# Gate scatter of a PEER layer: both gate parts side by side in one 256-column matmul, with PSUM divided anew for each stage

## Chip, cores, metric

One core of a Trainium2 chip runs the whole kernel. The metric is the device time of one execution in microseconds (us), as the median of several runs. Before the change it is 1055.61 us (three runs, 1055.03 to 1056.2).

## What is computed

The reference is one decoder layer on 256 tokens of width 1024: a mixing part (two attention branches, gated and merged), then a PEER part with 128 x 128 single-neuron experts, then a norm. Only the PEER part is touched:

```python
s = einsum('thpd,hpnd->thpn', qh, sub_keys)      # scores against 2 x 128 keys, 8 heads
sv, si = top_k(s, 16)                            # best keys, then best 16 pairs of them
expert_idx, gates = ...                          # 8 x 16 experts per token, softmax gates
hval = einsum('cd,chkd->chk', x, expert_u[expert_idx])
a = gates * gelu(hval)
out = einsum('chk,chkd->cd', a, expert_v[expert_idx])
```

## The kernel before

The kernel doesn't gather experts. It computes gelu(x @ u) for all 128 x 128 experts, multiplies by a matrix of gates that is zero where a token did not choose an expert, and multiplies the product by all of v. Experts are numbered (i, j); i counts 128 tiles, and j lies on the 128 partitions. Activations `act` are held as [j, i, token], in `act[0]` for i below N_PRE = 42 and in `act[1]` for the rest.

Products of full precision are made of three matmuls each (`mm3`, L93, L96, L97): both operands are split into a high part, rounded to fp32r, and the low rest. A weight block of 128 x 1024 comes by DMA into `raw`, ACT casts it to `hi` (L83), and DVE subtracts to get `lo` (L84); each has three buffers.

The stages in order: mixing part; the queries and scores of PEER (PQ, L573 to L585); the routing on DVE (`route`, top-k and index work), during which the first 42 up projections run; then the stage that matters here, the loop at L630 over i = 42 to 127; then the lower stage (`lower`, `v_step`, L655) with 12 matmuls of 512 columns for each of 128 blocks of v.

In the loop at L630 each i has one up projection (`up`, 24 matmuls of 256 columns into a PSUM tile `mm`) and `up_post`, which applies gelu: tokens that the scatter has not reached get the gelu written into `act` (L621), tokens that it has reached get it into `hg` (L624) and multiplied onto `act` (L625). In between, 64 calls of `scatter(t4, done)`, each for four tokens, are spread over the 86 values of i. A scatter builds the gate matrix of four tokens: `oh` (L602) holds one-hot rows of the expert numbers i and j, `gi` (L603) the one-hot of i times the gate, once for each of the two parts (high and low) into which a gate is split as f16. Both have the token innermost, so that one token's 128 columns are read in steps of four f16 elements. For each token, two matmuls of 128 columns (L606), one for each part, add up in PSUM, and give the gates as [j, i]. Four tokens fill one bank, a tile `tp`. DVE multiplies those of i below 42 onto `act[0]` (L608), those from 42 to `done` onto `act[1]` (L611), and ACT writes the others into `act[1]` (L613), where gelu will later be multiplied on.

PSUM has eight banks: four names (`mm`, `tp`, `sp`, `py`) with two each for the whole kernel. In the scatter stage `sp` and `py` lie idle; in the lower stage they are the four accumulators `acc`. At the lower stage's start ACT copies `ah` from `act` (L643) and DVE makes `al` (L644).

The order of instructions on each engine is set by the framework's scheduler, which goes by a modelled timeline; each engine then works through its queue strictly in order and waits on semaphores. All weight loads are issued on SP's queue; the change issues no DMA.

Of the kernel before, what the change touches and what calls it, by code (L numbers as in the profile page):

```python
# [9 lines left out]
F32 = mybir.dt.float32  # L10
F32R = mybir.dt.float32r
F16 = mybir.dt.float16
# [3 lines left out]
ALU = mybir.AluOpType  # L16
AX = mybir.AxisListType

P = 128
S = 256  # L20
# [9 lines left out]
NK = 128  # L30
# [9 lines left out]
G_SCALE = 2.0 ** 15  # L40
# [3 lines left out]
N_PRE = 42  # L44
# [7 lines left out]
def body(ctx, tc, x, g_mix, w_fb, w_va, w_qk, w_gate, w_f, b_f, w_br, w_out, g_ffn, w_pq,  # L52
         keys_t, u_t, v_e, g_fin, c_keep, c_mix, c_rot, c_sel, out, dbg=None):
    nc = tc.nc
# [4 lines left out]
    his = ctx.enter_context(tc.tile_pool(name="his", bufs=3))  # L59
    los = ctx.enter_context(tc.tile_pool(name="los", bufs=3))  # L60
    psum = ctx.enter_context(tc.tile_pool(name="psum", bufs=2, space=bass.MemoryType.PSUM))

    def bank(tag):
        return psum.tile([P, 512], F32, name=tag)

    def after(later, earlier):
        tc.add_manual_dep(
# [11 lines left out]
    def split(src, behind=None):  # L79
        r = load(src)  # L80
        h = his.tile([P, 1024], F32R, name="hi")
        l = los.tile([P, 1024], F32R, name="lo")
        ih = nc.scalar.copy(out=h, in_=r)  # L83
        il = nc.vector.tensor_tensor(out=l, in0=r, in1=h.bitcast(F32), op=ALU.subtract)  # L84
        lows.append(il)
        if behind is not None:
            for i, b in zip((ih, il), behind):
                if b is not None:
                    after(i, b)
        return h, l  # L90
# [25 lines left out]
    def norm_rstd(pool, src, tag, vector=(), cuts=(512, 1024)):  # L116

        rest = eps
        lo = 0
        for hi in cuts:  # L120
            ss = pool.tile([P, 1], F32, name="ss", bufs=8)
            piece = src[:, lo:hi]
            junk = bank(tag)[:, :hi - lo]
            if lo in vector:
                nc.vector.scalar_tensor_tensor(out=junk, in0=piece, scalar=1.0, in1=piece, op0=ALU.mult, op1=ALU.mult, accum_out=ss)
            else:
                nc.scalar.activation(out=junk, in_=piece, func=AF.Square, accum_out=ss)
            if hi < D:
                st = pool.tile([P, 1], F32, name="st", bufs=4)
                nc.vector.scalar_tensor_tensor(out=st, in0=ss, scalar=1.0 / D, in1=rest, op0=ALU.mult, op1=ALU.add)  # L130
                rest = st
            lo = hi
        sd = pool.tile([P, 1], F32, name="sd", bufs=4)
        nc.scalar.activation(out=sd, in_=ss, func=AF.Sqrt, scale=1.0 / D, bias=rest)
        rs = pool.tile([P, 1], F32, name="rs", bufs=4)
        nc.vector.reciprocal(out=rs, in_=sd)
        return rs
# [29 lines left out]
    def proj_t(src, xt, behind=None, tag="mm", late=False):  # L167
        w = split(src, behind)
        ps = bank(tag)[:, :S]
        if not late:  # L170
            for k in range(KD):
                mm3(ps, wk(w, k), [v[:, k] for v in xt], k == 0, k == KD - 1)
        else:

            for k in range(KD):
                for v in xt:
                    nc.tensor.matmul(ps, lhsT=wk(w, k)[0], rhs=v[:, k], start=k == 0 and v is xt[0], stop=False)  # L177
            for k in range(KD):
                nc.tensor.matmul(ps, lhsT=wk(w, k)[1], rhs=xt[0][:, k], start=False, stop=k == KD - 1)
        return ps  # L180


    with ExitStack() as fr:
# [5 lines left out]
        for t in range(NT):  # L189
            for n in range(2):  # L190
                sl = slice(n * 512, (n + 1) * 512)
# [23 lines left out]
        ps = bank("tp")[:HEADS, :S]  # L215
# [17 lines left out]
        for o in (0, 32, 64):  # L233
            part = ck[o:o + HEADS, P:]
# [6 lines left out]
        tp = bank("tp")  # L241
# [142 lines left out]
        for j2 in range(KD // 2):  # L384
# [3 lines left out]
            for jj in range(2):  # L388
                j = 2 * j2 + jj
                pp = []  # L390
                for w, yt, tag in ((wb, ys[0], "mm"), (wa, ys[1], "py")):
                    ps = bank(tag)[:, :S]
# [46 lines left out]
    ew = ctx.enter_context(tc.tile_pool(name="ew", bufs=2))  # L439
    pre = ctx.enter_context(tc.tile_pool(name="pre", bufs=1))  # L440
    act = [pre.tile([P, N_PRE, S], F32, name="act0")]

    def at(i):
        return act[0][:, i] if i < N_PRE else act[1][:, i - N_PRE]

    def up(i):
        ps = bank("mm")[:, :S]
        w = split(u_t[i])
        for k in range(KD):
            mm3(ps, wk(w, k), [a[:, k] for a in xt2], k == 0, k == KD - 1)  # L450
        return ps
# [99 lines left out]
    with ExitStack() as fr:  # L551
        tp_ = fr.enter_context(tc.tile_pool(name="tkp", bufs=1))
        tw = fr.enter_context(tc.tile_pool(name="tkw", bufs=2))
        kt = tp_.tile([P, 2 * PH * NK], F32, name="kt")
        nc.sync.dma_start(out=kt, in_=keys_t)
        val = tp_.tile([P, NT, 2 * PH, TOPK], F32, name="val")
        idx = tp_.tile([P, NT, 2 * PH, TOPK], U32, name="idx")
        scs = []
        steps = route(tp_, tw, val, idx, scs)
        debt = 0  # L560

        def spend(budget):
            nonlocal debt
            debt -= budget
            while debt < 0:
                c = next(steps, None)
                if c is None:
                    return False
                debt += c
            return True  # L570

        qhs = []
        for m in range(2 * PH):  # L573
            first = m < FIRST
            ps = proj_t(w_pq[m], xt2, (None if m == 0 else normed[0], normed[1]) if first else (qhs[m - FIRST], None), late=first)
            qh = tw.tile([P, S], F32, name="qh")
            qhs.append(nc.scalar.copy(out=qh, in_=ps))
            sp = bank("sp")[:, :NT * NK]
            for t in range(NT):
                nc.tensor.matmul(sp[:, t * NK:(t + 1) * NK], lhsT=qh[:, t * P:(t + 1) * P], rhs=kt[:, m * NK:(m + 1) * NK], start=True, stop=True)  # L580
            sc = tp_.tile([P, NT, NK], F32, name=f"sc{m}")
            nc.scalar.copy(out=sc, in_=sp.rearrange("p (t k) -> p t k", k=NK))
            scs.append(sc)
            if m > 0:
                spend(PQ_NS)  # L585

        for i in range(N_PRE):
            nc.scalar.activation(out=at(i), in_=up(i), func=AF.Gelu)  # L588
            spend(STEP_NS)
        for _ in steps:  # L590
            pass
    post = ctx.enter_context(tc.tile_pool(name="post", bufs=1))
    act.append(post.tile([P, NK - N_PRE, S], F32, name="act1"))

    def scatter(t4, done):

        ps = bank("tp")
        sl = slice(t4 * 4, t4 * 4 + 4)
        wide = [P, 2, NK, 4]
        oh = ew.tile(wide, F16, name="oh")  # L600
        gi = ew.tile(wide, F16, name="gi")
        nc.vector.tensor_tensor(out=oh, in0=iota.unsqueeze(1).to_broadcast(wide), in1=slot_e[:, :, sl].unsqueeze(2).to_broadcast(wide), op=ALU.is_equal)  # L602
        nc.vector.tensor_tensor(out=gi, in0=oh[:, 0].unsqueeze(1).to_broadcast(wide), in1=slot_g[:, :, sl].unsqueeze(2).to_broadcast(wide), op=ALU.mult)  # L603
        for q in range(4):
            for part in range(2):
                nc.tensor.matmul(ps[:, q * NK:(q + 1) * NK], lhsT=oh[:, 1, :, q], rhs=gi[:, part, :, q], start=part == 0, stop=part == 1)  # L606
        pv = ps.rearrange("p (q i) -> p i q", i=NK)
        nc.vector.scalar_tensor_tensor(out=act[0][:, :, sl], in0=pv[:, :N_PRE], scalar=1.0 / G_SCALE, in1=act[0][:, :, sl], op0=ALU.mult, op1=ALU.mult)  # L608
        d = done - N_PRE
        if d > 0:  # L610
            nc.vector.scalar_tensor_tensor(out=act[1][:, :d, sl], in0=pv[:, N_PRE:done], scalar=1.0 / G_SCALE, in1=act[1][:, :d, sl], op0=ALU.mult, op1=ALU.mult)  # L611
        if done < NK:
            nc.scalar.mul(out=act[1][:, d:, sl], in_=pv[:, done:], mul=1.0 / G_SCALE)  # L613

    last_gelu = []

# [13 lines left out]
    for i in range(N_PRE, NK):  # L630
        upto = -(-(i - N_PRE + 1) * n4 // (NK - N_PRE))
        while t4 < upto:
            scatter(t4, i)
            t4 += 1
        up_post(i, 4 * t4)

    acc = [[bank(tag) for _ in range(2)] for tag in ("py", "sp")]

    def lower(i):
        w = split(v_e[i])  # L640
        ah = ew.tile([P, S], F32R, name="ah", bufs=2)
        al = ew.tile([P, S], F32R, name="al", bufs=2)
        nc.scalar.copy(out=ah, in_=at(i))  # L643
        nc.vector.tensor_tensor(out=al, in0=at(i), in1=ah.bitcast(F32), op=ALU.subtract)  # L644
        return w, (ah, al)
# [49 lines left out]
    i = nc.vector.tensor_scalar(out=xg[0][:, halves[1]], in0=xg[0][:, halves[1]], scalar1=rs0, scalar2=None, op0=ALU.mult)  # L695
# [3 lines left out]
    for n, lo in enumerate((0, 256, 512, 768)):  # L699
        sl = slice(lo, lo + 256)  # L700
# [85 lines left out]
```

## Time and profile before

| | us |
|---|---|
| median of three runs | 1055.61 |
| the profiled execution | 1059.37 |
| its span, first to last instruction | 1057.6 |
| PE busy | 1040.5 |
| DVE busy | 740.6 |
| ACT busy | 546.1 |
| scatter stage, first to last scatter matmul | 388.5 to 696.7 |

PE is TensorE's matmuls, PEld its weight loads (they overlap with matmuls), DVE is VectorE, ACT ScalarE. Busy time is the union of an engine's instruction records. A matmul's record is longer than the distance between two matmuls, since they are pipelined; what one costs is read from the distance between starts, or from its share of the chain of waits over its count. The chain of waits is followed back from the end: at each step to what released an instruction or to the one before it on its engine. The granted clock of TensorE is 0.993 of full speed in the mean.

### The profile page before, as it was taken

How to read it: one execution, taken by the hardware profiler on the slowest of the kernel's cores; microseconds unless marked ns; L12 is line 12 of the kernel's file. 1: busy time of each engine (PE TensorE's matmuls, PEld its weight loads, DVE VectorE, ACT ScalarE, POOL GpSimd, SP SyncE). 2: the span in 40 equal slices, each digit the busy share in tenths (PEclk: the TensorE clock that was granted, in tenths of full speed). 3: DMA queues.
4: the chain of work that ended last, by engine and by line, in shares of the span. 5: the costliest groups of instructions: out<-in, count | busy, mean ns of one | idle time of the engine just before them, and what ended most of it. 6: DMA issues, size and time to landing. Idle time of an engine off the chain costs nothing.

```text
span 1057.6 us, 18493 instructions
## 1 busy us (share of the span) xinstructions
PE 1040.5 (98%) x7076; PEld 953.7 (90%) x7076; DVE 740.6 (70%) x1479; ACT 546.1 (52%) x983; POOL 6.9 (1%) x12
## 2 busy tenths in 40 slices
PE   7999999989999999999999999999999999999997
PEld 5888999989999999999999999998888888888886
DVE  4566546679999986677777788866566656656665
ACT  5555566454554544444444444455555555555554
POOL 1000000000000000000000000000000000000001
PEclk8999999999999999999999999999999999999999
DMA  6544435544566564545455444556666666666663
GB/s 206 172 139 118 123 120 175 186 169 151 167 190 189 177 186 150 158 142 155 146 151 149 146 152 142 157 163 197 189 193 198 192 190 195 196 190 193 198 193 126
DMA packets 49959, 177.84 MB, mean 168 GB/s; under 512 B 5752, under 2 KB 6648, under 8 KB 49744
## 3 DMA queue, kind: packets, MB, share of 16 engines
q1 hardware_dynamic: 49104, 175.62, 54.9%
q8 instruction: 55, 0.90, 0.4%
q10 hardware_dynamic: 432, 0.66, 0.2%
q0 software_dynamic: 336, 0.40, 0.2%
q14 instruction: 32, 0.26, 0.1%
HBM read 175.60 MB, written 1.05 MB: 167 GB/s over the span
## 4 chain that ended last, share of the span: by engine, by line
PE 95%; DVE 3%; DMA 1%; ACT 0%; issue 0%; SPq 0%; ACTq 0%
PE mm L93 16%; PE mm L96 15%; PE mm L97 15%; PE py L93 6%; PE py L97 6%; PE py L96 6%; PE tp L606 6%; PE sp L93 6%; PE sp L97 6%; PE sp L96 6%; PE sp L312 1%; PE mm L177 1%; DVE lo L84 1%; DMA cst<-in_c_keep_dram 1%; PE sp L580 1%; PE tp L327 1%
## 5 line engine op out<-in xcount | busy, mean ns | idle before, releaser
L84 DVE TENSOR_TENSOR lo<-raw,hi 128x1024 fp32r<-128x1024 f32 x328 | 400.2, 1221 | 145.7 <-ACT hi L83 143.8
L83 ACT CAST hi<-raw 128x1024 fp32r<-128x1024 f32 x328 | 344.8, 1053 | 256.2 <-PE mm L96 142.0
L93 PE MATMUL mm<-xt2h,hi 128*128 128x256 f32 x1128 | 325.8, 289 | 0.8 <-ACT act L588 0.8
L97 PE MATMUL mm<-xt2h,lo 128*128 128x256 f32 x1128 | 317.5, 281 | 0.5 <-DVE lo L84 0.5
L96 PE MATMUL mm<-xt2l,hi 128*128 128x256 f32 x1128 | 317.2, 281 | 0.0
L93 PEld LDWEIGHTS mm<-xt2h,hi 128*128 128x128 f32 x1128 | 214.3, 190 | 1.6 <-ACT act L588 1.0
L97 PEld LDWEIGHTS mm<-xt2h,lo 128*128 128x128 f32 x1128 | 212.7, 189 | 0.9 <-DVE lo L84 0.9
L96 PEld LDWEIGHTS mm<-xt2l,hi 128*128 128x128 f32 x1128 | 213.6, 189 | 0.0
L643 ACT CAST ah<-act 128x256 fp32r<-128x256 f32 x128 | 52.0, 407 | 95.2 <-PE sp L96 95.1
L644 DVE TENSOR_TENSOR al<-act,ah 128x256 fp32r<-128x256 f32 x128 | 54.3, 425 | 60.0 <-PE sp L97 59.1
L96 PE MATMUL py<-lo,ah 128*128 128x512 f32 x256 | 79.9, 390 | 0.0
L93 PE MATMUL py<-hi,ah 128*128 128x512 f32 x256 | 79.7, 390 | 0.0
L97 PE MATMUL py<-hi,al 128*128 128x512 f32 x256 | 79.6, 389 | 0.0
L96 PE MATMUL sp<-lo,ah 128*128 128x512 f32 x254 | 79.0, 389 | 0.0
L93 PE MATMUL sp<-hi,ah 128*128 128x512 f32 x254 | 78.9, 389 | 0.0
L97 PE MATMUL sp<-hi,al 128*128 128x512 f32 x254 | 78.7, 389 | 0.0
L606 PE MATMUL tp<-gi,oh 128*128 128x128 f16 x512 | 74.8, 296 | 0.0
L613 ACT ACTIVATE act<-tp 128x344 f32<-128x344 f32 (+31 forms) x64 | 20.3, 318 | 86.6 <-DVE act L611 80.8
L608 DVE SCALAR_TENSOR_TENSOR act<-tp,act 128x168 f32<-128x168 f32 x64 | 21.2, 332 | 56.1 <-PE tp L606 56.1
L93 PE MATMUL mm<-xt1h,hi 128*128 128x256 f32 x208 | 60.4, 290 | 0.0
L97 PE MATMUL mm<-xt1h,lo 128*128 128x256 f32 x208 | 59.5, 286 | 0.0
L96 PE MATMUL mm<-xt1l,hi 128*128 128x256 f32 x208 | 59.3, 285 | 0.0
(259 smaller groups left out, 1408.0 us busy)
## 6 DMA issues: line engine op xcount, KB each, us to landing
raw<-in_u_t_dram SPq DMA_DIRECT2D x128, 512.0 KB, 3.5
raw<-in_v_e_dram SPq DMA_DIRECT2D x128, 512.0 KB, 3.5
raw<-in_w_gate_dram SPq DMA_DIRECT2D x16, 512.0 KB, 3.6
raw<-in_w_pq_dram SPq DMA_DIRECT2D x16, 512.0 KB, 3.7
raw<-in_w_fb_dram SPq DMA_DIRECT2D x8, 512.0 KB, 4.7
raw<-in_w_va_dram SPq DMA_DIRECT2D x8, 512.0 KB, 3.5
raw<-in_w_qk_dram SPq DMA_DIRECT2D x8, 512.0 KB, 3.6
raw<-in_w_br_dram SPq DMA_DIRECT2D x8, 512.0 KB, 3.5
```

The source lines that it names most:

```text
L83: ih = nc.scalar.copy(out=h, in_=r)
L84: il = nc.vector.tensor_tensor(out=l, in0=r, in1=h.bitcast(F32), op=ALU.subtract)
L93: i = nc.tensor.matmul(ps, lhsT=lhs[0], rhs=rhs[0], start=start, stop=False)
L96: nc.tensor.matmul(ps, lhsT=lhs[0], rhs=rhs[1], start=False, stop=False)
L97: return nc.tensor.matmul(ps, lhsT=lhs[1], rhs=rhs[0], start=False, stop=stop)
L177: nc.tensor.matmul(ps, lhsT=wk(w, k)[0], rhs=v[:, k], start=k == 0 and v is xt[0], stop=False)
L312: nc.tensor.matmul(sp[:, o:o + n], lhsT=q[:, t * P:(t + 1) * P], rhs=k[:, :n], start=not fox, stop=not fox or t == 1)
L606: nc.tensor.matmul(ps[:, q * NK:(q + 1) * NK], lhsT=oh[:, 1, :, q], rhs=gi[:, part, :, q], start=part == 0, stop=part == 1)
L608: nc.vector.scalar_tensor_tensor(out=act[0][:, :, sl], in0=pv[:, :N_PRE], scalar=1.0 / G_SCALE, in1=act[0][:, :, sl], op0=ALU.mult, op1=AL ...
L613: nc.scalar.mul(out=act[1][:, d:, sl], in_=pv[:, done:], mul=1.0 / G_SCALE)
L643: nc.scalar.copy(out=ah, in_=at(i))
L644: nc.vector.tensor_tensor(out=al, in0=at(i), in1=ah.bitcast(F32), op=ALU.subtract)
```

## The change

Each token's two matmuls (128 columns each, adding up in PSUM) become one matmul of 256 columns: the left operand is the same, the right one is both parts of `gi` side by side, and the result lies in PSUM as two halves, `hi` and `lo`. So the tile of four tokens (`lay`) takes two banks. The halves are added while they are read: ACT copies the scaled low half to SBUF (`gl`), DVE adds the scaled high half, in `gl` for i below `done` and straight into `act[1]` for the rest, and then multiplies `gl` onto `act[0]` and `act[1]`.

The PSUM is divided by stage: `mm` and `tp` stay as they are; `sp` and `py` (four banks) are given up before the scatter stage, where two tiles `lay` take their place, and the lower stage opens four accumulators there again. `oh`, `gi` and `gl` lie in a pool of the scatter stage (`lw`), `ah` and `al` in one of the lower stage (`dw`); before they lay in `ew`, which was open from the routing on.

```diff
     psum = ctx.enter_context(tc.tile_pool(name="psum", bufs=2, space=bass.MemoryType.PSUM))
+    mixing = ExitStack()
+    psum2 = mixing.enter_context(tc.tile_pool(name="psum2", bufs=2, space=bass.MemoryType.PSUM))
     def bank(tag):
-        return psum.tile([P, 512], F32, name=tag)
+        return (psum2 if tag in ("sp", "py") else psum).tile([P, 512], F32, name=tag)
...
+    mixing.close()
     post = ctx.enter_context(tc.tile_pool(name="post", bufs=1))
+    laying = ExitStack()
+    lw = laying.enter_context(tc.tile_pool(name="lw", bufs=2))
+    psum3 = laying.enter_context(tc.tile_pool(name="psum3", bufs=2, space=bass.MemoryType.PSUM))
...
     def scatter(t4, done):
-        ps = bank("tp")
+        ps = psum3.tile([P, 4, 2, NK], F32, name="lay")
         sl = slice(t4 * 4, t4 * 4 + 4)
         wide = [P, 2, NK, 4]
-        oh = ew.tile(wide, F16, name="oh")
-        gi = ew.tile(wide, F16, name="gi")
+        oh = lw.tile(wide, F16, name="oh")
+        gi = lw.tile(wide, F16, name="gi")
...
         for q in range(4):
-            for part in range(2):
-                nc.tensor.matmul(ps[:, q * NK:(q + 1) * NK], lhsT=oh[:, 1, :, q], rhs=gi[:, part, :, q], start=part == 0, stop=part == 1)
-        pv = ps.rearrange("p (q i) -> p i q", i=NK)
-        nc.vector.scalar_tensor_tensor(out=act[0][:, :, sl], in0=pv[:, :N_PRE], scalar=1.0 / G_SCALE, in1=act[0][:, :, sl], op0=ALU.mult, op1=ALU.mult)
+            nc.tensor.matmul(ps[:, q], lhsT=oh[:, 1, :, q], rhs=gi[:, :, :, q], start=True, stop=True)
+        hi, lo = (ps[:, :, z].rearrange("p q i -> p i q") for z in range(2))
+        gl = lw.tile([P, NK, 4], F32, name="gl")
+        nc.scalar.mul(out=gl, in_=lo, mul=1.0 / G_SCALE)
         d = done - N_PRE
+        nc.vector.scalar_tensor_tensor(out=gl[:, :done], in0=hi[:, :done], scalar=1.0 / G_SCALE, in1=gl[:, :done], op0=ALU.mult, op1=ALU.add)
+        if done < NK:
+            nc.vector.scalar_tensor_tensor(out=act[1][:, d:, sl], in0=hi[:, done:], scalar=1.0 / G_SCALE, in1=gl[:, done:], op0=ALU.mult, op1=ALU.add)
+        nc.vector.tensor_tensor(out=act[0][:, :, sl], in0=gl[:, :N_PRE], in1=act[0][:, :, sl], op=ALU.mult)
         if d > 0:
-            nc.vector.scalar_tensor_tensor(out=act[1][:, :d, sl], in0=pv[:, N_PRE:done], scalar=1.0 / G_SCALE, in1=act[1][:, :d, sl], op0=ALU.mult, op1=ALU.mult)
-        if done < NK:
-            nc.scalar.mul(out=act[1][:, d:, sl], in_=pv[:, done:], mul=1.0 / G_SCALE)
+            nc.vector.tensor_tensor(out=act[1][:, :d, sl], in0=gl[:, N_PRE:done], in1=act[1][:, :d, sl], op=ALU.mult)
...
-    acc = [[bank(tag) for _ in range(2)] for tag in ("py", "sp")]
+    laying.close()
+    psum4 = ctx.enter_context(tc.tile_pool(name="psum4", bufs=2, space=bass.MemoryType.PSUM))
+    dw = ctx.enter_context(tc.tile_pool(name="dw", bufs=2))
+    acc = [[psum4.tile([P, 512], F32, name=tag) for _ in range(2)] for tag in ("py", "sp")]
     def lower(i):
         w = split(v_e[i])
-        ah = ew.tile([P, S], F32R, name="ah", bufs=2)
-        al = ew.tile([P, S], F32R, name="al", bufs=2)
+        ah = dw.tile([P, S], F32R, name="ah")
+        al = dw.tile([P, S], F32R, name="al")
```

## Rows read from the trace of the kernel before

**Rows 1.** The page: busy time by engine, and PE's slices in tenths.

```profile
PE 1040.5 (98%) x7076; PEld 953.7 (90%) x7076; DVE 740.6 (70%) x1479; ACT 546.1 (52%) x983; POOL 6.9 (1%) x12
...
PE   7999999989999999999999999999999999999997
```

**Rows 2.** Stretches of 50 us: length; busy PE, PEld, DVE, ACT, POOL; clock; DMA.

```profile
390.00:440.00 50.00, 50.00 (x424) 49.38 (x423) 32.88 (x62) 22.94 (x49) 0.00 (x0) 1.00 0.52 158
440.00:490.00 50.00, 50.00 (x423) 49.26 (x422) 36.20 (x72) 23.55 (x53) 0.00 (x0) 1.00 0.49 148
490.00:540.00 50.00, 50.00 (x424) 49.28 (x423) 36.34 (x69) 23.14 (x54) 0.00 (x0) 1.00 0.50 149
540.00:590.00 50.00, 50.00 (x423) 49.28 (x422) 38.70 (x72) 22.96 (x54) 0.00 (x0) 1.00 0.50 148
590.00:640.00 50.00, 50.00 (x424) 49.31 (x423) 38.58 (x69) 22.16 (x53) 0.00 (x0) 1.00 0.51 150
640.00:690.00 50.00, 50.00 (x424) 49.34 (x423) 41.39 (x72) 20.83 (x53) 0.00 (x0) 1.00 0.50 148
```

**Rows 3.** Chain of waits from 390 to 690 us, shares by line.

```profile
by line: PE mm L93 26.9%; PE mm L96 26.8%; PE mm L97 26.7%; PE tp L606 19.6%
```

**Rows 4.** Groups by line on PE, 390 to 690 us: busy, mean ns | idle.

```profile
L93 PE MATMUL mm<-xt2h,hi 128*128 128x256 f32 x681 | 198.5, 292 | 0.0
...
L606 PE MATMUL tp<-gi,oh 128*128 128x128 f16 x491 | 71.8, 296 | 0.0
```

**Rows 5.** Records of lines L606 and L200: ns min/median/max, first and last start.

```profile
L606 PEld LDWEIGHTS <-oh x512: 111/117/141, 388.4 to 696.6; 128*128 128x128 f16 x171
L606 PE MATMUL tp<-gi,oh x512: 280/297/303, 388.5 to 696.7; 128*128 128x128 f16 x171
...
L200 PE MATMUL py<-wz x14: 379/622/635, 1.2 to 5.9; 128*128 128x512 f16 x14
```

**Rows 6.** Timeline of PEld near 561 us: start us, length us.

```profile
561.17 0.35 PEld L606 LDWEIGHTS <-oh 128*128 128x128 f16 x4
```

**Rows 7.** A stretch of 100 us in the lower stage, columns as in rows 2.

```profile
800.00:900.00 100.00, 100.00 (x443) 82.85 (x442) 60.42 (x75) 53.87 (x74) 0.00 (x0) 1.00 0.64 192
```

**Rows 8.** Groups by line and shape, whole span: busy us, mean ns | idle before.

```profile
L608 DVE SCALAR_TENSOR_TENSOR act<-tp,act 128x168 f32<-128x168 f32 x64 | 21.2, 332 | 56.1 <-PE tp L606 56.1
...
L625 DVE TENSOR_TENSOR act<-act,hg 128x168 f32<-128x168 f32 x1 | 0.3, 323 | 0.0
...
L292 ACT COPY v<-mm 128x512 f32<-128x512 f32 x4 | 2.3, 586 | 2.4 <-PE mm L97 2.4
```

**Rows 9.** Timeline of DVE at the end of the scatter stage.

```profile
697.30 1.22 DVE L84 TENSOR_TENSOR lo<-raw,hi 128x1024 fp32r<-128x1024 f32 x1
698.44 0.50 DVE L611 SCALAR_TENSOR_TENSOR act<-tp,act 128x336 f32<-128x336 f32 x1
698.86 0.41 DVE L625 TENSOR_TENSOR act<-act,hg 128x252 f32<-128x252 f32 x1
699.18 0.42 DVE L644 TENSOR_TENSOR al<-act,ah 128x256 fp32r<-128x256 f32 x1
```

**Rows 10.** Waits from 390 to 690 us: us in total, times, longest.

```profile
DVE act L608 <- PE tp L606: 53.2, 57, 1.5
DVE lo L84 <- ACT hi L83: 21.2, 26, 2.3
```

**Rows 11.** Timelines of DVE and PE in the middle of the stage.

```profile
567.41 0.68 DVE L603 TENSOR_TENSOR gi<-oh,slot_g 128x1024 f16<-128x1024 f16 x1
...
571.61 1.11 PE L606 MATMUL tp<-gi,oh 128*128 128x128 f16 x8
```

**Rows 12.** Timelines of PE at the end of the scatter stage.

```profile
696.72 0.30 PE L606 MATMUL tp<-gi,oh 128*128 128x128 f16 x1
...
702.53 0.40 PE L93 MATMUL py<-hi,ah 128*128 128x512 f32 x1
```

**Rows 13.** Records of line L602.

```profile
L602 DVE TENSOR_TENSOR oh<-iota,slot_e x64: 675/681/693, 342.0 to 686.9; 128x1024 f16<-128x1024 f16 x64
```

## The prediction, made before the changed kernel ran

> **What bounds the kernel now.** I read the page first: PE is busy 98% of the span and DVE 70%, and PE's slices show no hole between start and end [rows 1]. A busy PE need not be a limiting PE, so next the stretches in which the scatter runs: from 390 to 690 us PE is busy 50.00 of every 50 us at full granted clock, while DVE climbs from 32.88 to 41.39 and ACT falls from 22.94 to 20.83 [rows 2]. Then the chain of waits there: it stays on PE throughout. The scatter matmuls (L606) own 19.6% of it, 58.8 us for 491 instructions, which is 119.8 ns each; the up projection's (L93, L96, L97, 2041 in all, 681 of them L93) own 80.4%, 118.2 ns each [rows 3, 4]. So time leaves this stage only through PE, and DVE has little room left before it is the next limit.
>
> **The matmuls.** Gone: 512 matmuls of 128 columns at 119.8 ns, 61.3 us of chain. New: 256 matmuls of 256 columns. Whether that halves the cost depends on what the 119.8 ns pay for.
> The weight load does not look like it. It is listed with 117 ns, but four loads in a row span 0.35 us, so the fourth starts 0.23 us after the first, 78 ns apart: they overlap, run ahead, and then wait for matmuls that come every 119.8 ns [rows 5, 6].
> Streaming does. A scatter matmul reads every fourth f16 element of gi, in steps of 8 bytes, and its 128 columns take as long as 256 dense columns of the up projection, 118.2 ns; its record has 297 ns, where a dense f16 one of 512 columns has 379 at best [rows 5]. A strided column seems to cost two dense ones. The nearest row for 256 strided columns is then the 512-column matmul of the lower stage: 443 in 100 us, 225.7 ns [rows 7]. Bounds: 119.8 ns if the old price buys 256 columns as well (30.7 us in all, a gain of 30.6), and twice 119.8 (no gain). I take 225.7 plus the 1.6 ns by which the strided one exceeds its dense twin, 227.3 ns: 58.2 us, **-3.1 us**. Per scatter that is 0.909 against 0.958, 0.05 us less.
> [...]
>
> **DVE.** L608 and L611 read PSUM and multiply in one pass. After, two sums read hi (512 elements together, split at "done"), and two multiplies read gl in SBUF, with the element counts of L608 and L611. The multiplies cost what the old passes did: 168 elements take 332 ns from PSUM (L608) and 323 from SBUF (L625) [rows 8]. The two sums come on top. L608 with 168 elements and L611 with 336 differ by 0.17 us, 1.0 ns per element; back to back L611 holds the engine 0.42 us (698.44 to 698.86), so about 0.08 is fixed [rows 8, 9]. The sums cost 512 x 1.0 ns + 2 x 0.08 = **0.67 us** per scatter, 43 us over 64. Bounds: 0.59 (one fixed part hidden) and 0.84 (both paid at record length, 332 - 168 ns fixed).
> What covers them is DVE's idle time. 491 matmuls in 300 us are 10.2 scatters per 50 us, so DVE gets 6.9 us more in each stretch: 39.8, 43.1, 43.2, 45.6, 45.5, 48.3. PE needs 50 - 10.2 x 0.05 = 49.5. Even the last stretch fits, with 1.2 us to spare: **0**, but the cover is nearly used up.
>
> **ACT and the new wait.** L613 becomes one copy of 512 elements from PSUM, 586 ns by L292 [rows 8]; even with nothing taken off for L613 that is 6 us per stretch in an engine idle for 26 us or more of every 50 [rows 2]: 0. New is that DVE waits for ACT's gl, where L608 waited for PE (53.2 us in all, 0.86 per scatter) [rows 10]. Behind the waiting sum on DVE stand oh, the next lo and gi, and PE waits for lo and gi. On ACT gl and the hi casts stand in one queue, so either can hold the other for one cast. Today gi is ready well ahead: made from 567.41 to 568.09, its eight matmuls start at 571.61 [rows 11]. These 3.5 us pay for single late sums: 0 here; the other end is the second rival.
>
> **Pools, and the end of the stage.** The PSUM that lay takes was last read in the PQ stage, before the routing: 0. acc and ah now wait until the last scatter lets go. Before, the last scatter matmul starts at 696.72, al runs from 699.18 to 699.60, and PE reaches the first lower matmul at 702.53 [rows 9, 12]. The copy (0.59) and two sums (0.67) move al's end to 700.9, and with one more lo in front (698.44 minus its start at 697.30, 1.14) to 702.0 [rows 9]: still in time, 0; bound 1 us. oh and gi move to a pool opened after the routing, where the first oh was made at 342 us [rows 13]. If two pairs must now come after it, some 2.7 us of DVE leave the crowded routing stretch for the first scatter stretch, which has 9.7 to spare: 0, within 1 us either way.
>
> **Sum.** The profiled execution took 1059.4 us, its span 1057.6; the median of the runs shown is 1055.6, 3.8 below it. 1059.4 - 3.1 + 0 + 0 + 0 = 1056.3; carried to the median, **1052.5 us**. A measurement of this kernel tells about 0.2% (2.1 us) from no change.
>
> **The rivals.**
> *Gain eaten, no change.* If each scatter's sum still waits 0.35 us for gl, DVE needs 3.6 us more per 50: the last stretch misses by 2.4 us, and with a stage end 0.5 us late the gain is gone: 1055.4. The same comes out at 239.6 ns per matmul. For it: lo alone waits 21.2 us for hi already [rows 10]. Against it: DVE waits today because it is ahead.
> *DVE becomes the limit, slower.* The place is the first sum of each scatter, in order behind PE and ACT. It decides from some 0.38 us of wait per scatter on, where the fourth and fifth stretch are full too (3.9 us / 10.2). At 0.6 us (6.1 per stretch) the last three miss by 2.2, 2.1 and 4.9 us: 9.2 - 3.1, 1061.7. With today's 0.86 kept, some 1075. For it: 48.3 of 49.5 late in the stage, and one engine more in the chain. Against it: a DVE that is late finds gl done.
> *The stride is free, much faster.* At 119.8 ns PE needs 45.1 us per old 50, and DVE takes over in the last three stretches (45.6, 45.5, 48.3): 25 us saved, 1030; with 0.35 us of wait per scatter 11 us, 1044; I name 1036. Against it stands that 128 strided columns cost what 256 dense ones do. [...]
>
> **How the numbers follow.** Forecast 1052.5, chance 0.42 (own range 1051 to 1054); gain eaten 0.26; DVE the limit 0.22; free stride 0.10. A twentieth, from the first, lands inside 0.2%: faster 0.47, same 0.31, slower 0.22. The range holds the first two whole and the DVE case up to 0.6 us of wait, and goes down to 1046 for a stride that is only partly dear (a fifth of the way to the far bound); the free stride (0.10) and the far DVE tail (0.07) are left out: 1046 to 1062.
>
> **What would show it.** Right: the new matmuls come about 227 ns apart, PE is busy 50 of 50 from 390 us to the stage's end, DVE near 45 in the mean and 48 late, and its waits for gl are short. Wrong: PE idle before L93 or L97 with DVE's lo as releaser, or before the scatter matmuls with gi; matmuls 120 ns apart; a hole on PE near 700 us.

## The result, and the profile after

The changed kernel takes **1073.11 us** (median of four runs, 1071.78 to 1074.59) against 1055.32 for the kernel before beside it: a ratio of **1.0167, 95% interval [1.0155, 1.018]**, slower by 17.8 us. That lies outside the range of 1046 to 1062. The profiled execution took 1074.59 us, its span 1072.6.

The page of the changed kernel, as in [rows 1]: PE's busy share is the same 98%, with 256 matmuls fewer, and DVE has 41.5 us more. Line numbers shift by the change: L93, L96 and L97 become L95, L98 and L99, the scatter matmul L606 becomes L611, `oh` is L608, `gl` L614, the two sums are L616 and L618, the two multiplies L619 and L621, the gelu L629 and L632.

```profile
PE 1052.4 (98%) x6820; PEld 936.1 (87%) x6820; DVE 782.1 (73%) x1607; ACT 559.7 (52%) x983; POOL 6.9 (1%) x12
```

The stretches, with the columns of [rows 2, 7] (length; busy PE, PEld, DVE, ACT, POOL; clock; DMA), show three places:

```profile
390.00:440.00 50.00, 50.00 (x386) 46.26 (x386) 40.06 (x85) 25.50 (x53) 0.00 (x0) 1.00 0.54 167
...
540.00:590.00 50.00, 50.00 (x386) 46.44 (x385) 43.66 (x88) 25.63 (x55) 0.00 (x0) 1.00 0.51 156
590.00:640.00 50.00, 48.34 (x368) 43.88 (x366) 43.95 (x86) 24.23 (x51) 0.00 (x0) 1.00 0.49 150
640.00:690.00 50.00, 48.27 (x363) 43.70 (x364) 44.85 (x87) 23.27 (x50) 0.00 (x0) 1.00 0.45 138
690.00:720.00 30.00, 26.39 (x144) 22.46 (x144) 18.52 (x35) 14.16 (x25) 0.00 (x0) 0.89 0.38 122
...
800.00:900.00 100.00, 100.00 (x432) 81.09 (x431) 59.00 (x73) 52.52 (x72) 0.00 (x0) 1.00 0.60 188
```

*The lower stage.* PE is busy without a gap at full clock, as before, and yet only 432 matmuls start in 100 us where 443 did [rows 7]: 231.5 ns each for 225.7. Over the stage's 1536 matmuls these 5.8 ns make 8.9 us, half of the loss, in a stage whose matmuls the change doesn't touch.

*The late scatter stage.* From 590 to 690 us PE has 3.4 us of idle time, where it had none. *The end of that stage.* From 690 to 720 us 3.6 us are missing, and the mean granted clock is 0.89 (it was 1.00 before). The waits from 385 to 720 us (us in total, times, longest):

```profile
DVE oh L608 <- PE lay L611: 32.1, 49, 1.5
DVE lo L86 <- ACT hi L85: 13.6, 20, 1.9
ACT gl L614 <- PE lay L611: 11.2, 7, 3.4
...
ACT gl L614 <- DVE act L621: 5.5, 5, 1.3
...
PE mm L95 <- ACT hg L632: 3.6, 5, 1.0
PE py L95 <- ACT ah L654: 3.4, 1, 3.4
```

The two PE waits are new. The first is the up projection waiting for a PSUM tile `mm` that gelu has not read. ACT's timeline there (start us, length us, idle before) shows why gelu is late:

```profile
630.48 0.21 ACT L629 ACTIVATE act<-mm 128x56 f32<-128x56 f32 x1
630.59 0.59 ACT L614 ACTIVATE gl<-lay 128x512 f32<-128x512 f32 x1
633.35 1.05 ACT L85 CAST hi<-raw 128x1024 fp32r<-128x1024 f32 x1 [2.17 <-PE mm L98]
634.30 0.21 ACT L629 ACTIVATE act<-mm 128x52 f32<-128x52 f32 x1
634.41 0.59 ACT L614 ACTIVATE gl<-lay 128x512 f32<-128x512 f32 x1
634.89 0.33 ACT L632 ACTIVATE hg<-mm 128x200 f32<-128x200 f32 x1
```

One tile's gelu is in two parts: 56 tokens at 630.48 and the other 200 at 634.89, 4.4 us later, with two `gl` and a `hi` that waits for PE in between. `mm` has two buffers, so PE stops (0.96 us there, until 635.28).

The second wait is the hole before the first lower matmul. DVE's timeline:

```profile
700.96 0.68 DVE L616 SCALAR_TENSOR_TENSOR gl<-lay,gl 128x504 f32<-128x504 f32 x1
701.55 0.15 DVE L618 SCALAR_TENSOR_TENSOR act<-lay,gl 128x8 f32<-128x8 f32 x1
703.58 1.22 DVE L86 TENSOR_TENSOR lo<-raw,hi 128x1024 fp32r<-128x1024 f32 x1 [1.88 <-ACT hi L85]
704.73 0.33 DVE L619 TENSOR_TENSOR act<-gl,act 128x168 f32<-128x168 f32 x1
704.97 0.50 DVE L621 TENSOR_TENSOR act<-gl,act 128x336 f32<-128x336 f32 x1
```

and PE's:

```profile
702.30 0.28 PE L99 MATMUL mm<-xt2h,lo 128*128 128x256 f32 x1
706.02 0.79 PE L95 MATMUL py<-hi,ah 128*128 128x512 f32 x1 [3.43 <-ACT ah L654]
706.61 0.63 PE L98 MATMUL py<-lo,ah 128*128 128x512 f32 x1
707.03 0.63 PE L95 MATMUL py<-hi,ah 128*128 128x512 f32 x1
```

The last scatter's sums are done at 701.7, but a `lo` for the lower stage stands between them and the multiplies. It waits 1.88 us for its `hi` (which waits 1.95 us for a buffer that PE reads up to its last up projection), so the multiplies end at 705.5, and `ah` needs them. After 3.43 us of idle time the lower stage starts at half the granted clock (0.50 from 706.0 to 711.7 us, where it was 1.00 from 690 to 702): its first matmuls are 0.43 us apart, up to 711.7, and 0.23 later.

### The profile page after: what moved, and what is told of

The parts are those of the page before. It is cut to its first block, busy times and chain, and to the rows that moved or that the text cites. A ratio compares the mean times of both kernels' runs of the same rounds, so it can differ in the third digit from the quotient of the medians.

```text
span 1072.6 us, 18119 instructions
## 1 busy us (share of the span) xinstructions
PE 1052.4 (98%) x6820; PEld 936.1 (87%) x6820; DVE 782.1 (73%) x1607; ACT 559.7 (52%) x983; POOL 6.9 (1%) x12
## 5 line engine op out<-in xcount | busy, mean ns | idle before, releaser
L95 PE MATMUL mm<-xt2h,hi 128*128 128x256 f32 x1128 | 328.5, 291 | 3.6 <-ACT hg L632 3.6
L98 PE MATMUL mm<-xt2l,hi 128*128 128x256 f32 x1128 | 318.1, 282 | 0.0
L99 PE MATMUL mm<-xt2h,lo 128*128 128x256 f32 x1128 | 318.1, 282 | 0.0
L95 PEld LDWEIGHTS mm<-xt2h,hi 128*128 128x128 f32 x1128 | 213.6, 189 | 11.9 <-ACT hg L632 5.8
L98 PEld LDWEIGHTS mm<-xt2l,hi 128*128 128x128 f32 x1128 | 213.6, 189 | 1.6
L99 PEld LDWEIGHTS mm<-xt2h,lo 128*128 128x128 f32 x1128 | 212.8, 189 | 0.7
L95 PE MATMUL py<-hi,ah 128*128 128x512 f32 x256 | 81.9, 398 | 3.4 <-ACT ah L654 3.4
L98 PE MATMUL py<-lo,ah 128*128 128x512 f32 x256 | 81.7, 397 | 0.0
L99 PE MATMUL py<-hi,al 128*128 128x512 f32 x256 | 81.0, 396 | 0.0
L98 PE MATMUL sp<-lo,ah 128*128 128x512 f32 x254 | 80.7, 396 | 0.0
L95 PE MATMUL sp<-hi,ah 128*128 128x512 f32 x254 | 80.7, 396 | 0.0
L99 PE MATMUL sp<-hi,al 128*128 128x512 f32 x254 | 80.2, 396 | 0.0
L611 PE MATMUL lay<-gi,oh 128*128 128x256 f16 x256 | 69.5, 407 | 0.0
L608 DVE TENSOR_TENSOR oh<-iota,slot_e 128x1024 f16<-128x1024 f16 x64 | 44.1, 690 | 32.3 <-PE lay L611 32.1
L95 PEld LDWEIGHTS py<-hi,ah 128*128 128x128 f32 x256 | 48.7, 190 | 15.0 <-ACT ah L654 3.6
L95 PE MATMUL mm<-xt1h,hi 128*128 128x256 f32 x208 | 60.4, 290 | 0.0
L99 PE MATMUL mm<-xt1h,lo 128*128 128x256 f32 x208 | 59.5, 286 | 0.0
L98 PE MATMUL mm<-xt1l,hi 128*128 128x256 f32 x208 | 59.2, 285 | 0.0
```

What stands on the lines that cost most here:

```text
L95: i = nc.tensor.matmul(ps, lhsT=lhs[0], rhs=rhs[0], start=start, stop=False)
L98: nc.tensor.matmul(ps, lhsT=lhs[0], rhs=rhs[1], start=False, stop=False)
L99: return nc.tensor.matmul(ps, lhsT=lhs[1], rhs=rhs[0], start=False, stop=stop)
L611: nc.tensor.matmul(ps[:, q], lhsT=oh[:, 1, :, q], rhs=gi[:, :, :, q], start=True, stop=True)
```

## The experiments

Fourteen kernels ran; e1, e8 and e11 to e14 were timed four times or more, the others once. The first three asked for the lower stage. In the diffs `...` stands for lines not shown.

**e1.** Before, with `ah` and `al` alone moved to a pool of their own above everything else, as the change places them.

```diff
+    dw = ctx.enter_context(tc.tile_pool(name="dw", bufs=2))
...
-        ah = ew.tile([P, S], F32R, name="ah", bufs=2)
-        al = ew.tile([P, S], F32R, name="al", bufs=2)
+        ah = dw.tile([P, S], F32R, name="ah")
+        al = dw.tile([P, S], F32R, name="al")
```

> The kernel before, with one thing of the change: ah and al lie in a pool opened after act1, so at the top of SBUF (byte 224384 of a partition on) in place of 92672. In the changed kernel the lower stage's matmuls of 512 columns come 231.4 ns apart (432 to 433 in 100 us), before 225.7 (443). Theory A (where ah and al lie sets that pace): 432 to 434 matmuls in 100 us of the lower stage, some 8 us slower in all, about 1063.5. Theory B (the accumulators' PSUM banks) and theory C (something the scatter stage leaves behind, or the single execution): 442 to 444 in 100 us, the time of before.

1063.77 us, ratio 1.0074 [1.0057, 1.009]. The stretch in the lower stage:

```profile
800.00:900.00 100.00, 100.00 (x432) 81.09 (x431) 59.05 (x73) 52.22 (x72) 0.00 (x0) 1.00 0.63 188
```

This edit alone brings the 432, and costs 7.6 us over the kernel before measured beside it (1056.13). So about half of the loss is where two small tiles lie in SBUF.

**e2.** Before, with `sp` and `py` in a PSUM pool of their own, opened as in the changed kernel, which moves `py` to other banks.

```diff
+    psum2 = ctx.enter_context(tc.tile_pool(name="psum2", bufs=2, space=bass.MemoryType.PSUM))
...
-        return psum.tile([P, 512], F32, name=tag)
+        return (psum2 if tag in ("sp", "py") else psum).tile([P, 512], F32, name=tag)
```

> The kernel before, with another single thing of the change: sp and py in a PSUM pool of their own, which moves the accumulators py from banks 0 and 1 to banks 4 and 5, as in the changed kernel. Theory A (place of ah and al): 443 matmuls in 100 us of the lower stage. Theory B (PSUM banks): 432 to 434.

1054.04 us, 443 matmuls per 100 us: the banks change nothing.

**e3.** The changed kernel, with `ah` and `al` in the space of `xt2[0]`, at a low address (17888 bytes on). The pool `dw` is left out.

```diff
-        ah = dw.tile([P, S], F32R, name="ah")
-        al = dw.tile([P, S], F32R, name="al")
+        ah = xt2[0][:, i % 2]
+        al = xt2[0][:, 2 + i % 2]
```

> The changed kernel, with ah and al written into the space of xt2, which the lower stage no longer needs (bytes 17888 to 21984 of a partition), in place of 216192 on. Theory A: 442 to 444 matmuls in 100 us of the lower stage, 8 us less than the changed kernel, about 1064 to 1066 (a little more is lost at the stage's start, since ah must wait for the last up projection). Theories B and C: 432 to 434, the time of the changed kernel.

1074.09 us and 430 per 100 us: as slow at a low address. That low is fast was wrong; it isn't the region.

**e5, e6 and e7** tried the address modulo 512 bytes. Before, `ah` lies at 92672, a multiple of 512; in the changed kernel at 216192, in e1 at 224384 and in e3 at 17888, which are not. e5 is e1 with 384 bytes of padding (224768, a multiple); e6 is before with 128 bytes of padding (92800, not one); e7 is the changed kernel with 384 bytes (216576, a multiple).

```diff
+    nc.gpsimd.memset(dw.tile([P, 96], F32, name="pad", bufs=1), 0.0)
```

> As e1 (the kernel before with ah and al in a pool at the top of SBUF), with 384 unused bytes in front of them in the pool: they start at byte 224768, a multiple of 512, in place of 224384, which is only one of 128. The fast placement so far, 92672, is a multiple of 512; the three slow ones (216192, 224384, 17888) are not. Theory A1 (the start's multiple of 512 bytes counts): 442 to 444 matmuls in 100 us of the lower stage, time as before, about 1055. Theory A2 (the region of SBUF counts): 430 to 434, about 1063.

1055.58 us: padding alone takes e1's loss away. Its stretch:

```profile
800.00:900.00 100.00, 100.00 (x442) 82.79 (x442) 60.71 (x74) 53.71 (x74) 0.00 (x0) 1.00 0.66 194
```

> The kernel before with 128 unused bytes in front of ah in its old pool: ah and al start at 92800, no multiple of 512, in the old region. Theory A1: 430 to 434 matmuls in 100 us of the lower stage, about 1063. Theory A2: 442 to 444, about 1055.

1063.42 us: padding alone brings the loss to the kernel before. Its stretch:

```profile
800.00:900.00 100.00, 100.00 (x432) 81.07 (x431) 59.05 (x73) 52.50 (x72) 0.00 (x0) 1.00 0.64 189
```

> The changed kernel with 384 unused bytes in front of ah and al, which then start at 216576, a multiple of 512. Theory A1: 442 to 444 matmuls in 100 us of the lower stage, and some 8 us less than the changed kernel, 1064 to 1066; what is left over the kernel before (9 us) is then the stage's end and the waits for ACT. Theory A2: 430 to 434, no gain.

1064.35 us, 443 per 100 us: some 8.8 us of the change's 17.8 are the address of `ah` and `al`. All addresses tried so far that are fast are multiples of 512, and all slow ones are 128 or 480 past one; whether a smaller multiple would do was not tried. Some 9 us are left, in the scatter stage and at its end.

**e4** asked what the scatter matmul pays for. It is the changed kernel, whose matmuls read 256 neighbouring elements of `gi` in place of every fourth one; the gates land in wrong places.

```diff
+        gd = gi.rearrange("p z i q -> p (z i q)")
...
-            nc.tensor.matmul(ps[:, q], lhsT=oh[:, 1, :, q], rhs=gi[:, :, :, q], start=True, stop=True)
+            nc.tensor.matmul(ps[:, q], lhsT=oh[:, 1, :, q], rhs=gd[:, q * 2 * NK:(q + 1) * 2 * NK], start=True, stop=True)
```

> The changed kernel, with the right operand of the scatter matmul read as 256 neighbouring f16 elements in place of every fourth one (so the gates land in wrong places); nothing else moves. Theory S (the stride of 8 bytes halves the streaming): the scatter matmuls come 110 to 120 ns apart in place of 227, each four of them take 0.45 us, and the stage from 390 us on is up to 27 us shorter where PE bounds it. Theory W (the strided weight load, which stays, sets the pace): still 220 ns or more.

1042.35 us, with the slow lower stage and all. The scatter stage ends at 671 us in place of 702. Two stretches:

```profile
540.00:590.00 50.00, 50.00 (x425) 49.56 (x425) 48.41 (x98) 27.57 (x59) 0.00 (x0) 1.00 0.54 167
590.00:640.00 50.00, 46.84 (x392) 45.59 (x390) 47.17 (x92) 25.57 (x54) 0.00 (x0) 1.00 0.49 151
```

Four scatter matmuls of one call, in the changed kernel and here:

```profile
441.70 1.09 PE L611 MATMUL lay<-gi,oh 128*128 128x256 f16 x4
```

```profile
442.33 0.63 PE L612 MATMUL lay<-gi,oh 128*128 128x256 f16 x4
```

Less the last one's record (407 and 280 ns in the mean), three distances are left: 228 ns each before this edit, 117 with it. The weight load keeps its steps of 8 bytes in both. So the stride of the moving operand sets the price of the scatter matmul, as the prediction argued. DVE reaches 48.4 of 50 here, and then PE waits.

**e8** uses this without the change: the kernel before, with two tokens innermost in `oh` and `gi`, so that a token's columns lie 4 bytes apart and not 8, in the stationary `oh` as well as in the moving `gi`. `gi` is made in two DVE operations. The core of it:

```diff
-        wide = [P, 2, NK, 4]
-        oh = ew.tile(wide, F16, name="oh")
-        gi = ew.tile(wide, F16, name="gi")
+        oh = ew.tile([P, 2, 2, NK, 2], F16, name="oh")
+        gi = ew.tile([P, 2, 2, NK, 2], F16, name="gi")
...
-                nc.tensor.matmul(ps[:, q * NK:(q + 1) * NK], lhsT=oh[:, 1, :, q], rhs=gi[:, part, :, q], start=part == 0, stop=part == 1)
+                nc.tensor.matmul(ps[:, q * NK:(q + 1) * NK], lhsT=oh[:, q // 2, 1, :, q % 2], rhs=gi[:, part, q // 2, :, q % 2], start=part == 0, stop=part == 1)
```

> The kernel before with only the layout of oh and gi changed: two tokens innermost in place of four, so that a token's 128 columns are read in steps of 4 bytes in place of 8 (gi then takes two DVE instructions of 512 elements). Theory S (a step of 8 bytes halves the streaming): if 4 bytes are read at full rate, the scatter matmuls come 55 to 75 ns apart in place of 119.8, up to 30 us less on PE, with DVE at some 45 of each (shorter) 50 us; 1026 to 1035. Theory S with any step being dear, or a cost of the short matmul by itself: still 118 to 120 ns, time as before or 1 to 3 us more.

**1028.88 us, ratio 0.975 [0.9729, 0.9771]**: faster than both kernels by far. The scatter matmul's share of the chain from 390 to 640 us, and its group in the same stretch:

```profile
by line: PE mm L93 30.7%; PE mm L96 29.2%; PE mm L97 29.2%; PE tp L611 10.9%
```

```profile
L611 PE MATMUL tp<-gi,oh 128*128 128x128 f16 x454 | 39.4, 221 | 0.0
```

10.9% of 250 us over 454 are 60.0 ns, half of the 119.8 of [rows 3, 4]: 512 x 59.8 ns = 30.6 us, and the gain is 27.1. The rest is found on L93, the line of the first matmul behind each scatter: 30.7% over its 617 matmuls are 124.4 ns each, where L96 and L97 cost 118.2 and L93 cost 118.5 in the kernel before, some 4 us over the stage. The layout is worth far more than the merging of two matmuls, which e13 below puts at 1 to 2 us.

**e9, e10 and e11** mend what e7 left. e9 makes two moves at once: it puts that `lo` of the lower stage behind the last scatter's multiply, and ACT's table load (1.28 us, at 703.85 in the changed kernel, ahead of `ah`) behind the third `ah`; e10 lets every second up projection take its PSUM tile from `tp`, idle in this stage, so that four buffers stand where two did; e11 does both.

```diff
-        w = split(v_e[i])
+        w = split(v_e[i], (None, last_mult[0]) if i == 2 else None)
...
-    warm_sqrt(last_gelu[-1])
+    warm_sqrt(copies[2])
```

```diff
-        ps = bank("mm")[:, :S]
+        ps = bank("tp" if i >= N_PRE and i % 2 else "mm")[:, :S]
```

> The changed kernel with ah and al at multiples of 512 bytes (1064.35 us in its one look), and two orders at the stage's end: the third lo of the lower stage comes after the last scatter's multiply on DVE, and the load of ACT's table after the third ah. Theory H (the hole before the first lower matmul is made by that lo, which waits for hi and stands ahead of the multiplies, and by the table load ahead of ah): the hole of 3.4 us shrinks under 0.5 us, the granted clock from 690 to 720 us stays at 1.00 in place of 0.89, and about 5.5 us go: 1058 to 1060. Rival (the sums and multiplies are late by themselves, the order matters little): the hole keeps over 2 us and the time stays at 1063 to 1065.

1059.57 us, 4.8 less than e7. The hole shrank to 1.6 us, where under 0.5 was forecast, but the clock stayed up (1.00, in e7 0.89). Its waits on PE and its last stretch:

```profile
PE mm L95 <- ACT hg L635: 3.6, 5, 1.0
PE py L95 <- ACT ah L658: 1.6, 1, 1.6
```

```profile
690.00:720.00 30.00, 28.23 (x159) 24.07 (x158) 20.45 (x36) 16.86 (x28) 0.18 (x1) 1.00 0.54 157
```

> The changed kernel with ah and al at multiples of 512 bytes (1064.35 us), with the up projection's PSUM tile taken by turns from mm and from tp, which lies idle in the scatter stage, so that four buffers stand where there were two. Theory G (PE stands still for 3.4 us from 590 to 690 us because the gelu that reads mm stands behind hi and gl in ACT's queue, and both mm are full): PE is busy over 49.7 of 50 us in these stretches, and the time falls by 2.5 to 4 us, to 1060 to 1062, with the hole at the stage's end still there. Rival (ACT and DVE are late anyway, the wait only changes its place, to lo or gi): PE loses as much elsewhere, and the time stays within 1 us of 1064.

1064.27 us, no gain. The waits on PE:

```profile
PE py L95 <- ACT ah L655: 6.3, 1, 6.3
PE tp L95 <- ACT hg L632: 1.0, 1, 1.0
```

The stall inside the stage went from 3.6 to 1.0, and the hole grew from 3.4 to 6.3. PE arrives earlier and waits longer: buffers only moved the wait.

> The changed kernel with all three mended: ah and al at multiples of 512 bytes, the order at the stage's end, and four buffers for the up projection. If the three places hold the whole loss (8.8, some 5.5, some 3), what is left is the matmul term that the prediction forecast, 3.1 us less than before: 1052 to 1055 against 1055.3 for the kernel before, a ratio of 0.997 to 1.000. If something else is lost as well, the time stays above 1058.

1060.45 us, ratio 1.0046 [1.003, 1.0063]: above 1058, so something else is lost. Its waits on PE are 3.6 us before the lower stage and 1.0 inside, and the clock is low again behind the hole, for a shorter time than in the changed kernel:

```profile
690.00:720.00 30.00, 26.39 (x131) 21.52 (x131) 21.30 (x39) 15.77 (x27) 0.18 (x1) 0.94 0.45 138
```

In DVE's timeline from 693.2 to 701.6 some 0.5 us are without work; its first and last lines there, and ACT's `ah`, which waits for the last multiply:

```profile
693.21 0.69 DVE L610 TENSOR_TENSOR oh<-iota,slot_e 128x1024 f16<-128x1024 f16 x1 [0.21 <-PE lay L613]
...
701.25 0.41 DVE L636 TENSOR_TENSOR act<-act,hg 128x256 f32<-128x256 f32 x1
```

```profile
701.36 0.71 ACT L658 CAST ah<-act 128x256 fp32r<-128x256 f32 x2 [0.28 <-DVE act L623]
```

**e13** takes the two sums away from e11. ACT copies the scaled high half into `gl` and `act`; the low half of the gates is not added. Matmuls, the way through `gl` and the multiplies stay.

```diff
-        nc.scalar.mul(out=gl, in_=lo, mul=1.0 / G_SCALE)
-        nc.vector.scalar_tensor_tensor(out=gl[:, :done], in0=hi[:, :done], scalar=1.0 / G_SCALE, in1=gl[:, :done], op0=ALU.mult, op1=ALU.add)
+        nc.scalar.mul(out=gl[:, :done], in_=hi[:, :done], mul=1.0 / G_SCALE)
         if done < NK:
-            nc.vector.scalar_tensor_tensor(out=act[1][:, d:, sl], in0=hi[:, done:], scalar=1.0 / G_SCALE, in1=gl[:, done:], op0=ALU.mult, op1=ALU.add)
+            nc.scalar.mul(out=act[1][:, d:, sl], in_=hi[:, done:], mul=1.0 / G_SCALE)
```

> The changed kernel with all three mended (1060.45 us), and with the two sums left out: ACT copies the scaled high half into gl for i below done and into act for the rest, and the low half of the gates is not added, so the gates have the precision of one f16 part. The matmuls, the waits through gl and the multiplies stay; about 0.67 us of DVE per scatter, 43 us, are gone. Theory D (these sums are what is late: DVE has no cover left near the stage's end): DVE falls to 37 to 40 of 50 us, the PE waits inside the stage and the 3.6 us before the lower stage fall under 1 us together, and about 6 us go: 1053 to 1055. Rival C (the chain PE, ACT, DVE is late by its length, whatever DVE has to do): the hole before the lower stage keeps over 2 us and the time stays at 1058 to 1061.

1053.95 us, ratio 0.9987 [0.9978, 0.9997]: 6.5 less than e11 (6.1 when each is set against the kernel before measured beside it), and PE has no wait left from 390 to 720 us. That is what e11 lost: 3.6 and 1.0 us of waits, and some 1.7 us by the lower clock (0.94 of 30 us). Two stretches, DVE's longest waits from 390 to 720 us, and the scatter matmuls' group and the chain from 390 to 690 us:

```profile
640.00:690.00 50.00, 50.00 (x386) 46.35 (x385) 40.49 (x69) 25.94 (x67) 0.00 (x0) 1.00 0.49 152
690.00:720.00 30.00, 30.00 (x165) 25.93 (x164) 18.91 (x28) 17.23 (x30) 0.18 (x1) 1.00 0.59 179
```

```profile
DVE oh L610 <- PE lay L613: 53.6, 60, 1.5
DVE lo L86 <- ACT hi L85: 31.1, 37, 2.0
```

```profile
L613 PE MATMUL lay<-gi,oh 128*128 128x256 f16 x244 | 66.1, 406 | 0.0
```

```profile
by line: PE lay L613 18.9%; PE mm L98 14.0%; PE mm L95 14.0%; PE mm L99 14.0%; PE tp L95 13.1%; PE tp L98 13.0%; PE tp L99 13.0%
```

DVE is ahead of PE again, as before the change (53.6 us of waiting for the scatter matmuls, all of it before 690 us; 53.2 in [rows 10]). ACT's queue has mended itself too: both parts of a gelu now stand together.

```profile
632.57 0.21 ACT L631 ACTIVATE act<-mm 128x56 f32<-128x56 f32 x1
632.68 0.33 ACT L634 ACTIVATE hg<-mm 128x200 f32<-128x200 f32 x1
```

So what is late in e11 is DVE, by the sums; the way through ACT (the rival C) by itself costs nothing that these times show. The scheduler orders ACT's queue by its own model of when DVE is done, so the price of the sums holds that order too: the runs don't part the two.

**e14** keeps the sums in e11 and ends the scatters four up projections earlier.

```diff
-        upto = -(-(i - N_PRE + 1) * n4 // (NK - N_PRE))
+        upto = min(n4, -(-(i - N_PRE + 1) * n4 // (NK - N_PRE - 4)))
```

> The changed kernel with all three mended (1060.45 us), with the 64 scatters spread over 82 values of i in place of 86, so that the last four up projections (11 us of PE) stand behind the last scatter. Theory P (only the place of the last scatters is wrong; DVE has enough time over the whole stage): the hole before the lower stage goes, and the time falls by some 5 us to 1054 to 1057. Theory D (DVE has no cover left): DVE's work is packed 5% tighter, 47 to 48 of 50 us, PE waits inside the stage for what it did not wait at the end, and the time stays within 2 us of 1060.

1061.66 us, ratio 1.0067 [1.005, 1.0084]. The hole before the lower stage is gone, and PE waits inside the stage in its place:

```profile
PE tp L95 <- ACT hg L635: 3.4, 4, 1.0
PE mm L95 <- ACT hg L635: 2.9, 3, 1.0
```

Again the wait changed its place. In all it is 7.0 us in e7, 5.2 in e9, 7.3 in e10, 4.6 in e11 and 6.3 here: an order at the stage's end takes away a part of it, and of all that was tried only less work for DVE (e13) removed it.

**e12** put a question to e8: is the moving operand's address worth something as well? `xt2` moves from 17888 to 17920 bytes, a multiple of 512, with padding of 32 bytes ahead of it and 480 behind, so that all else but `x2`, which lies between them and is no operand of these matmuls, keeps its place modulo 512.

```diff
+    nc.gpsimd.memset(keep.tile([P, 8], F32, name="padlo"), 0.0)
...
+    nc.gpsimd.memset(keep.tile([P, 120], F32, name="padhi"), 0.0)
```

> The kernel before with two tokens side by side in oh and gi (1028.88 us), and with xt2, the moving operand of the up projection, moved from an address of 17888 bytes to 17920, a multiple of 512. If the start of a moving operand matters as that of the stationary one of 512 columns does, the up projection's matmuls fall below 118.2 ns, by up to 2.9 ns in the ratio of the lower stage's (231.3 to 225.7), 3072 of them, up to 9 us: 1020 to 1027. If only the stationary operand's start matters, 1028 to 1030.

1033.42 us, ratio 0.9786 [0.977, 0.9802]: 4.5 slower than e8 (3.8 by the two ratios). Its chain from 390 to 640 us:

```profile
by line: PE mm L93 30.8%; PE mm L96 29.3%; PE mm L97 29.2%; PE tp L613 10.8%
```

The share of the up projection is 89.3% of 250 us over 1836 matmuls, 121.6 ns, where e8 has 89.1% over 1852, 120.3 ns (both with the dearer first matmul behind a scatter); 1.3 ns x 3456, all matmuls that read `xt2`, are the 4.5 us. L96 and L97 alone, without that first matmul, are 119.5 ns here and 118.2 in e8 (58.5% of 250 us over 1224, 58.4% over 1235); in e11, run beside e12 with `xt2` in its old place, 43 distances between starts from 689.59 to 696.08 us have 118.1 in the mean. Neither forecast held: the address matters here too, in the other direction. Why is open.

## Why the prediction was wrong

The forecast of 1052.5 missed by 20.6 us. Set against the kernel before that was measured beside each run, e7 is 8.4 us slower, e11 5.1 slower and e13 1.0 faster. So the 17.8 us of loss are: the address of `ah` and `al`, +9.4 (the change less e7; e1, four runs, has 7.6 for it, and the count of matmuls 8.9); the order at the stage's end and the buffers of the up projection together, +3.3 (e7 less e11); the two sums on DVE, +6.1 (e11 less e13); what is then left of the change, -1.0 (e13). e7 ran once, so the two terms that use it are good to about 1 us. Read from the trace of the changed kernel instead, the loss is 8.9 for the address, 7.0 of PE's waits and 2.5 of lower clock, less 1.8 for the matmuls, together 16.6; the other 1.2 us have no place there.

- *The matmuls, -3.1: the mechanism held, the size was off.* 18.9% of 300 us over 244 records in e13 are 232.4 ns for 256 columns, not 227.3: a gain of (239.6 - 232.4) x 256 = 1.8 us. The 232.4 lies about midway between the lower stage's 225.7 and twice 119.8. Why it is 5.1 ns above the forecast is open: `oh` and `gi` too went from multiples of 512 bytes (82432 and 86528 on) to 128 past one (216192 and 220288 on), and no run of the changed kernel put them back. That streaming of 8-byte steps and not the weight load sets the price is shown by e4, where only the moving operand's steps change; e8, where both operands' do, agrees: 128 columns go at 60.0 ns in steps of 4 bytes (e8) and at 119.8 in steps of 8 (before). A free stride of 8 bytes, 119.8 ns for 256 columns, is shown by no run (228 ns in the changed kernel, 232.4 in e13); that rival was rightly held unlikely for this change.
- *"Pools, and the end of the stage ... 0; bound 1 us": this step failed, and worst.* The pools were looked at for what must wait for what, and never for where the tiles come to lie. `ah` and `al` in a new pool start 128 bytes past a multiple of 512, and that costs some 8 to 9 us; no rival had it. At the end itself, the estimate of 702.0 for `al` put one more `lo` in front of it but not that `lo`'s own wait for `hi`. The `lo` went between sums and multiplies, `ah` came at 705.56, and the hole took the clock with it (0.89 in the mean from 690 to 720 us).
- *"Even the last stretch fits ... 0": this step failed too.* The 0.67 us per scatter are right: DVE's busy time grew from 740.6 to 782.1, 0.65 us per scatter. That the sum fits into idle time is right as well (44.9 of 50 us late in the stage, 48.3 forecast). Yet the sums cost 6.1 us, which e13 gives back. The forecast took DVE's idle time as free to use; what is left of it in the changed kernel from 385 to 720 us is mostly waiting for PE's matmuls (32.1 us) and for `hi` (13.6), and at the stage's end DVE has a backlog, which the next stage waits for. That DVE's lateness is the cause is shown; that its in-order waits are why 45 of 50 us is already too much is argued. "The cover is nearly used up" was the line to follow.
- *"ACT and the new wait ... 0 here": right for the wait that it named, blind to another.* DVE's sums do not wait for `gl` (no such row among DVE's waits). ACT waits for DVE instead: `gl` for L621, 5.5 us. The 3.5 us by which `gi` was ready were no cover for `mm`, which is released by ACT.
- *The rivals.* "DVE becomes the limit" had the right engine and nearly the right price (9.2 at 0.6 us of wait; 6.1 measured), but the wrong place: not the first sum's wait for `gl`, but the multiplies and `hg` that come late behind the sums. With the address added, the time went past the range's upper end. The agreement in price is luck, since the wait that it was worked out from is not there. "Gain eaten" did not come, nor did the matmul at 239.6 ns.
- *The signs named in advance.* "A hole on PE near 700 us" was seen. PE idle before L93 (here L95) was seen too, but not with DVE's `lo` as releaser, as the sign had it: ACT's `hg`, which frees `mm`, came last. The sign of the largest loss, the lower stage's count of matmuls, was not on the list.

## What to carry to other kernels

When a change opens or moves a memory pool, compare the start addresses of every operand of the main matmuls before and after, not only the lifetimes, and look at the matmul count of stages that the change doesn't touch. Work added to an engine that is busy 41 of 50 us next to the limit isn't free because it fits: its idle time can already belong to waits, and a backlog falls due where the stage ends. Test it by taking the work away, since here added buffers only moved the wait, and other orders took away a part of it. And when a short matmul costs as much as one twice as wide (here 119.8 ns for 128 columns and 118.2 for 256), mend the layout that it reads before merging matmuls: two tokens innermost in place of four gave 2.5%, with less added work than the change.

## What the hardware showed that was not expected

- A stationary fp32r operand of 128 columns whose tile starts 128 bytes past a multiple of 512 slows matmuls of 512 columns from 225.7 to 231.5 ns, at the full granted clock (e1, e5, e6, e7); 480 bytes past one (e3) did the same (430 in 100 us), other offsets weren't tried. With the moving operand of the up projection the aligned address was the slower one, 121.6 against 120.3 ns by the chain, 119.5 against 118.2 without the first matmul behind a scatter (e12, e8); that is not explained.
- A moving f16 operand in steps of 8 bytes streams 128 columns in 119.8 ns (before) and 256 in 232.4 (e13, its operands 128 bytes past a multiple of 512); in steps of 4 bytes, in both operands, it streams 128 in 60.0 ns (e8), and without steps 256 in 117 (e4).
- After an idle time of PE of 3.43 us the first 13 matmuls of the lower stage ran at a granted clock of 0.50 (706.0 to 711.7 us), most of them 427 ns apart, a loss of some 2.5 us in all; after one of 3.61 us (e11) the low stretch was shorter (granted clock 0.94 from 690 to 720 us, where it was 0.89), and after one of 1.6 us (e9) the clock stayed at 1.00.
